# Decode scores: which cached row and which query stand on which partition

## The chip, the cores and the metric

The kernel runs on one core of a Trainium2 chip. The metric is the device time of one execution in microseconds (us); lower is better. A core has five engines that run side by side: TensorE (PE in the profile, its weight loads PEld), VectorE (DVE), ScalarE (ACT), GpSimd (POOL) and SyncE (SP). Each engine takes its instructions in one fixed order, and a waiting instruction holds everything behind it. In this kernel SP issues all data transfers, which 16 DMA engines carry out.

## What is computed

The reference is one inference step of a hybrid layer: a prompt of 1024 rows, and 8 decode requests of 4 new rows each, with 1024 cached key and value rows per request. The part that the change touches is the attention of the new rows to the cache:

```
DILATED_PATTERNS = ((128, 1), (512, 4), (2048, 16))
def _dilated_gather(q, k_all, v_all, window, dil):
    offs = jnp.arange(window // dil + 1) * dil
    idx = (l_ - t_ + jnp.arange(t_))[:, None] - offs[None, :]
    ...
    s = jnp.einsum('bthe,btkhe->bhtk', q, kg) * (HEAD_DIM ** -0.5)
    ...
    o = jnp.einsum('bhtk,btkhe->bthe', p, vg)
def _sample_attention(q, k, v, k_past, v_past):
    ...
    return _combine([_dilated_gather(q, k_all, v_all, w, d) for w, d in DILATED_PATTERNS])
```

Query j (0 to 3) sees keys at distances 0, d, 2d and so on, so with a dilation of 4 or 16 each of the four queries has cached rows of its own: rows j, j+4, j+8, ... among the last 512, and rows j, j+16, ... among the first 512.

## The kernel before

**Stages.** About the first 100 us load and normalise the input. Up to about 320 us the state-space branch runs, with blocks of the input projection between its steps. From 320 to about 540 us come the gated unit of that branch (PE line 748, DVE lines 754 and 755, ACT lines 753, 757 and 759, POOL line 760), the decode scores against the cached keys, and the last three blocks of the input projection (6, 10 and 11; PE line 313, 144 multiplications each; a block's weights come by line 219 and are split by ACT line 141 and DVE line 142). From about 542 us the prompt attention runs, with the decode values and the output projection between its steps, and the rest is the last output projection and the final norm.

**Decode scores.** A loop over the 8 requests (line 818) loads for each request b six tiles of 128 partitions by 512 floats, 256 KB each:

- line 791, tile 0: the last 128 cached key rows. PE transposes it (line 822) and multiplies it with all four queries (lines 828 and 829).
- line 835, `dq`: the four queries of the request, each repeated on 32 partitions.
- line 793, tile 1: the rows of dilation 16, four query classes of 32 rows.
- line 797, tiles 6 to 9: the rows of dilation 4, four query classes of 32 rows in each tile.

Tiles 1 and 6 to 9 go to `dot`: POOL multiplies the tile with `dq` (line 802), and DVE sums each head's 64 products into `scd` (line 803). `query j` has to stand in `dq` on the partitions on which its own rows stand in the tile: before, query j is on partitions 32j to 32j+31.

**Buffers.** The cached tiles share three buffers (`ct`), `dq` has one. So the load of a tile waits until the tile three places ahead of it has been used, and the load of the next request's queries waits until the fifth product of this request is done. All loads, and the stores of other stages, stand in SP's one order.

**What follows.** When all of `scd` is there, PE transposes it (lines 914 and 929), DVE copies it into `sc` in the order query by key (lines 921 and 931), a softmax runs over it (lines 958 to 969), PE turns the weights back (lines 979 and 1008), and the constant `sel3` (line 1543) keeps on each partition only the query that belongs there. The decode values (`values_ops`) load the cached value rows with the same function `cache_tile`: lines 791, 793 and 795.

**What sets the order.** Up to line 866 a scheduler of the framework orders each engine's instructions from estimated durations; from line 868 on a planner (`Plan`) does so with costs and due times written in the code. Waits are fixed when the program is built.

## Time and profile before

| | us |
|---|---|
| median of 3 runs | 816.28 |
| lowest and highest | 814.58, 818.41 |
| the profiled execution's own time | 816.68 |
| its span in the trace | 814.8 |

The profile is of one execution. A row of an engine tells where it was busy and what released it after it had been idle; "DMA ct<-in_cache_k_dram" as a releaser means that the transfer of a cached key tile landed last. In windows, the DMA share is the mean busy share of the 16 DMA engines. The granted clock is TensorE's: 1.00 is 2.4 GHz, 0.50 is 1.2 GHz. Times are counted from the span's start. The chain of waits follows the work that ended last back through what released it; a DMA piece in it lasts from issue to landing.

### The profile page before, as it was taken

Reading aid. Unit: us, or ns where it says so; the run is one execution under the profiler, and the core shown is the slowest. Engines: PE = TensorE matmul, PEld = TensorE weight load, DVE = VectorE, ACT = ScalarE, POOL = GpSimd, SP = SyncE. Lnnn points to the kernel's source line nnn. Section 1 sums busy time; section 2 is a strip of 40 time slices with the busy share of each in tenths; the row PEclk is TensorE's granted clock in tenths of the full one; section 3 lists DMA queues with packets and bytes.
Section 4 is the critical chain, followed back from the end, with each engine's and each line's share of the span. In section 5 each row is a group of like instructions: output and inputs, shape, how many; then the busy total and the mean of one; then the engine's idle time right before and its main releaser. Section 6 shows DMA issues by size and latency. Waiting matters only on the chain.

```text
span 814.8 us, 12780 instructions
## 1 busy us (share of the span) xinstructions
PE 703.5 (86%) x4286; PEld 634.6 (78%) x4286; DVE 561.2 (69%) x1249; ACT 363.3 (45%) x814; POOL 347.0 (43%) x315
## 2 busy tenths in 40 slices
PE   7999989598989999587767668989989999989996
PEld 6999878588978899576767657867757777778896
DVE  5995787879786762444435355649789999996286
ACT  6653244223425244322212222228667787772163
POOL 2506663544654410133433334016567687740022
PEclk9999999798999999796898878989999999999999
DMA  8424142322332444554434354368898788305423
GB/s 282 162 79 139 37 135 85 119 63 67 110 123 93 156 132 147 151 143 160 127 119 142 114 175 139 108 183 243 251 254 247 218 234 242 101 6 181 132 84 130
DMA packets 77362, 118.38 MB, mean 145 GB/s; under 512 B 14544, under 2 KB 42704, under 8 KB 77296
## 3 DMA queue, kind: packets, MB, share of 16 engines
q1 hardware_dynamic: 77296, 117.56, 46.8%
q8 instruction: 34, 0.56, 0.3%
q14 instruction: 32, 0.26, 0.1%
HBM read 85.73 MB, written 30.62 MB: 143 GB/s over the span
## 4 chain that ended last, share of the span: by engine, by line
PE 37%; DMA 28%; DVE 17%; issue 5%; ACT 5%; POOL 4%; SPq 3%; DVEq 0%; POOLq 0%; ACTq 0%
DMA ct<-in_cache_k_dram 13%; PE mm L313 13%; PE mm L293 4%; DMA ct<-in_cache_v_dram 4%; PE ss L293 3%; PE tp L293 3%; PE fo L1418 3%; DMA wst<-in_w_in_dram 3%; PE so L684 2%; POOL dm L802 2%; DVE pm L1269 2%; PE ops L1323 2%; DVE vl L1107 2%; DMA dq<-d_pd 2%; DVE pl L1315 2%
## 5 line engine op out<-in xcount | busy, mean ns | idle before, releaser
L313 PE MATMUL mm<-xT,win 128*128 128x352 f32 x1440 | 262.9, 338 | 23.4 <-DVE eq L380 16.7
L313 PEld LDWEIGHTS mm<-xT,win 128*128 128x128 f32 x1440 | 242.4, 198 | 28.0 <-issue 14.6
L802 POOL TENSOR_TENSOR dm<-ct,dq 128x512 f32<-128x512 f32 x40 | 52.5, 1312 | 124.2 <-DMA ct<-in_cache_k_dram 80.4
L803 DVE TENSOR_REDUCE scd<-dm 128x8 f32<-128x512 f32 x40 | 27.4, 684 | 78.0 <-POOL dm L802 78.0
L748 PE MATMUL ss<-yh,wg 128*128 128x272 f32 (+1 forms) x256 | 56.4, 317 | 19.8 <-DVE z L754 17.1
L1289 POOL TENSOR_SCALAR pm<-pm,rd 128x128 f32<-128x128 f32 (+3 forms) x64 | 52.0, 818 | 39.1 <-DVE rd L1285 27.6
L748 PEld LDWEIGHTS ss<-yh,wg 128*128 128x128 f32 x256 | 46.5, 217 | 22.4 <-DVE z L754 18.7
L142 DVE SCALAR_TENSOR_TENSOR win<-wst,gin,win 128x256 fp32r<-128x256 f32 x96 | 55.2, 617 | 11.0 <-ACT win L141 10.7
L141 ACT ACTIVATE win<-wst,gin 128x256 fp32r<-128x256 f32 x96 | 43.7, 502 | 33.7 <-DMA wst<-in_w_in_dram 29.8
L1281 ACT ACTIVATE pm<-pm,mn 128x128 f32<-128x128 f32 (+3 forms) x64 | 49.2, 770 | 15.3 <-DVE mn L1269 14.9
L1315 DVE TENSOR_TENSOR pl<-tp,ph 128x512 fp32r<-128x512 f32 (+1 forms) x80 | 49.7, 628 | 5.7 <-ACT ph L1312 5.4
L1418 PE MATMUL fo<-wo,gh 128*128 128x512 f32 x192 | 51.1, 408 | 0.0
L293 PE MATMUL mm<-win,xT 128*128 128x256 f32 x384 | 50.4, 286 | 0.1
L1308 PE MATMUL tp<-ident,pm 128*128 128x128 f32 x288 | 47.0, 283 | 1.5 <-DVE mn L1269 1.2
L293 PEld LDWEIGHTS mm<-win,xT 128*128 128x128 f32 x384 | 46.9, 189 | 0.5 <-ACT xT L138 0.4
L1312 ACT ACTIVATE ph<-tp 128x512 fp32r<-128x512 f32 (+1 forms) x80 | 42.9, 543 | 2.7 <-PE tp L1308 1.2
L1269 DVE CUSTOM_DVE_ANT_0 pm<-ss,maskp 128x512 f32<-128x512 f32 (+2 forms) x64 | 36.9, 580 | 9.6 <-DMA qt<-d_q 4.8
L1266 PE MATMUL ss<-ka,qt 128*128 128x512 f32 (+2 forms) x96 | 38.1, 398 | 4.3 <-DMA ka<-d_k 2.4
L1308 PEld LDWEIGHTS tp<-ident,pm 128*128 128x128 f32 x288 | 35.6, 145 | 7.5 <-DVE mn L1269 1.9
L1418 PEld LDWEIGHTS fo<-wo,gh 128*128 128x128 f32 x192 | 35.4, 194 | 6.6
L1103 ACT ACTIVATE vh<-ct 128x512 fp32r<-128x512 f32 x48 | 30.0, 626 | 23.1 <-DMA ct<-in_cache_v_dram 10.9
L379 ACT ACTIVATE eq<-mm 64x352 fp32r<-64x352 f32 (+1 forms) x48 | 21.5, 448 | 41.7 <-DVE eq L380 20.6
(399 smaller groups left out, 1584.7 us busy)
## 6 DMA issues: line engine op xcount, KB each, us to landing
wst<-in_w_in_dram SPq DMA_DIRECT2D x24, 512.0 KB
ct<-in_cache_k_dram SPq DMA_DIRECT2D x48, 256.0 KB
ct<-in_cache_v_dram SPq DMA_DIRECT2D x48, 256.0 KB
xt<-in_x_prompt_dram SPq DMA_DIRECT2D x8, 512.0 KB
wst<-in_w_out_dram SPq DMA_DIRECT2D x8, 512.0 KB
xres<-in_x_prompt_dram SPq DMA_DIRECT2D x8, 512.0 KB
qt<-d_q SPq DMA_DIRECT2D x16, 256.0 KB
qw<-d_q SPq DMA_DIRECT2D x32, 128.0 KB
```

The lines of the kernel that those rows point to most:

```text
L141: S.activation(hi, src, AF.Copy, scale=scale)
L142: V.scalar_tensor_tensor(lo, src, scale, f(hi), op0=OP.mult, op1=OP.subtract)
L293: T.matmul(out, lhs(a, kt), w(b, kt)[:, c0:c0 + cn], start=(n == 0), stop=(n == 3 * ktn - 1))
L313: T.matmul(p, w(b, kt)[:, c * 128:c * 128 + 128], x(a, kt), start=(n == 0), stop=(n == 23))
L748: T.matmul(p, wg[:, b, kt, c:c + 128], yT[a][:, kt, :, :w], start=(i == 0), stop=(i == 11))
L802: GP.tensor_tensor(out=m, in0=kt, in1=qt, op=OP.mult)
L1269: V.tensor_tensor_reduce(out=x.pm[:, 512 * c:512 * c + w], in0=x.p[c][:, :w], in1=maskp[:, (7 - i) * 128 + 512 * c:(7 - i) * 128 + 512 * c ...
L1281: S.activation(x.pm[:, :n], x.pm[:, :n], AF.Exp, scale=-1.0, bias=x.mn[:, nch - 1:nch], accum_out=x.dn)
L1289: a = op(PO, 0.02 + n * 0.0012, lambda: GP.tensor_scalar(x.pm[:, :n], x.pm[:, :n], x.rd, 1.0, op0=OP.mult, op1=OP.mult), pr, [a], give=["rd"])
L1308: T.transpose(x.p[:, n * 128:n * 128 + 128], o.rows[2 * m + u].pm[:, j * 128:j * 128 + 128], ident)
L1315: V.tensor_tensor(out=x.l[:, :w], in0=x.p[:, :w], in1=f(x.h[:, :w]), op=OP.subtract)
L1418: T.matmul(o.f[hf], o.g[u][:, i, k], wo[0][:, j, 2 * u + k, hf * 512:hf * 512 + 512], start=(u + k + n == 0), stop=(u + k + n == 4))
```

## The change

The partitions are renumbered: query j now stands on partitions 4m+j instead of 32j+m. With that,

- line 797 loads the 128 consecutive cached rows of a tile (rows 512+128i to 639+128i for tile 6+i) one after the other, where it loaded the same 128 rows as four classes of 32, each row four rows after the one before it;
- line 793 loads the same 128 rows as before, with the 32 groups m outermost and the class j inside, for the keys and for the values;
- line 835 loads the queries as 32 repeats of the group of four, where it loaded four groups of 32 repeats;
- the copies out of the transposes (lines 920, 928 to 931) and one copy ahead of line 1008 (line 1012) step through their input or output with a stride of four elements, and `sel3` follows.

Number and size of the transfers, the shapes of all instructions on the engines, and the arithmetic are as before. Since the scheduler orders the stage from estimated durations, instructions of the stage stand in another order; outside 320 to 540 us the order on each engine is the same.

```diff
         elif t == 1:
-            SY.dma_start(c, src[b, 0:512, :].rearrange("(m r) c -> r m c", r=16)[0:DS])
+            SY.dma_start(c, src[b, 0:512, :].rearrange("(m r) c -> m r c", r=16)[:, 0:DS])
...
         else:
-            SY.dma_start(c, src[b, 512:1024, :].rearrange("(m r j) c -> m j r c", r=32, j=DS)[t - 6])
+            SY.dma_start(c, src[b, 128 * t - 256:128 * t - 128, :])
...
-        SY.dma_start(qt, d_pd[:, b, 1024:1536].unsqueeze(1).to_broadcast([DS, 32, 512]))
+        SY.dma_start(qt, d_pd[:, b, 1024:1536].unsqueeze(0).to_broadcast([32, DS, 512]))
...
-                out, p = out.rearrange("q j (m r) -> q m j r", r=32), (lambda: o.p.rearrange("q m (j r) -> q m j r", r=32))
+                out, p = out.rearrange("q j (m r) -> q m j r", r=32), (lambda: o.p.rearrange("q m (r j) -> q m j r", j=DS))
...
-            o.p = fo_ps([64, 4, 32])
-            T.transpose(o.p.rearrange("p j m -> p (j m)"), scd[:, 8].rearrange("p b h -> p (b h)"), ident)
+            o.p = fo_ps([64, 32, 4])
+            T.transpose(o.p.rearrange("p m j -> p (m j)"), scd[:, 8].rearrange("p b h -> p (b h)"), ident)
...
-        step(VE, 0.2, lambda: V.tensor_scalar(sc[:, :, 256:288], o.p, 0.125, 0.0, op0=OP.mult, op1=OP.add), give=["fo"])
+        step(VE, 0.2, lambda: V.tensor_scalar(sc[:, :, 256:288], o.p.rearrange("p m j -> p j m"), 0.125, 0.0, op0=OP.mult, op1=OP.add), give=["fo"])
...
-            V.tensor_copy(o.s3.rearrange("p (j m) -> p j m", j=4), sc[:, :, 256:288])
+            V.tensor_copy(o.s3.rearrange("p (m j) -> p j m", j=4), sc[:, :, 256:288])
...
-    sel3 = (np.arange(128)[:, None] // 32 == np.arange(4)[None, :]).astype(np.float32)
+    sel3 = (np.arange(128)[:, None] % 4 == np.arange(4)[None, :]).astype(np.float32)
```

**SP, the loads of the third request.** `ct` are the cached tiles, `dq` the queries, `gt` a gate tile of the gated unit (line 740), `d_k<-eq` a store of block 6. Before:

```order
L793 DMA ct_4541<-in_cache_k_dram 128x1x512
L381 DMA d_k_84<-eq_4871 128x320
L835 DMA dq_4539<-d_pd_91 128x1x512
L797 DMA ct_4546<-in_cache_k_dram 128x1x512
L381 DMA d_k_84<-eq_4900 128x352
L740 DMA gt_4087<-d_gs_88 128x2x128
L381 DMA d_k_84<-eq_4904 128x352
L797 DMA ct_4551<-in_cache_k_dram 128x1x512
L797 DMA ct_4556<-in_cache_k_dram 128x1x512
L740 DMA gt_4120<-d_gs_88 128x2x128
L797 DMA ct_4561<-in_cache_k_dram 128x1x512
L791 DMA ct_4566<-in_cache_k_dram 128x512
```

After:

```order
L793 DMA ct_4541<-in_cache_k_dram 128x1x512
L740 DMA gt_4087<-d_gs_88 128x2x128
L835 DMA dq_4539<-d_pd_91 128x1x512
L797 DMA ct_4546<-in_cache_k_dram 128x512
L381 DMA d_k_84<-eq_4900 128x352
L381 DMA d_k_84<-eq_4904 128x352
L740 DMA gt_4120<-d_gs_88 128x2x128
L797 DMA ct_4551<-in_cache_k_dram 128x512
L797 DMA ct_4556<-in_cache_k_dram 128x512
L740 DMA gt_4154<-d_gs_88 128x2x128
L797 DMA ct_4561<-in_cache_k_dram 128x512
L791 DMA ct_4566<-in_cache_k_dram 128x512
```

The gate tiles stand one place earlier against the cached tiles, and the cached tiles of line 797 have the plain form of line 791's.

**PE, the transposes of the last request's tile 0** (`ct_4762`), between the multiplications of block 10 (`mm`). Before:

```order
L313 MATMUL mm_5122<-xT0_97,win_5088 128x352 x2
L313 MATMUL mm_5122<-xT1_98,win_5088 128x352
L822 MATMUL tp_4764<-ident_73,ct_4762 128x128 x4
L763 MATMUL so_3782<-ones_69,acc_4230 128x1 x2
L313 MATMUL mm_5151<-xT0_97,win_5067 128x352 x2
```

After:

```order
L313 MATMUL mm_5210<-xT1_98,win_5076 128x352
L313 MATMUL mm_5210<-xT0_97,win_5079 128x352
L822 MATMUL tp_4764<-ident_73,ct_4762 128x128 x4
L313 MATMUL mm_5210<-xT0_97,win_5079 128x352
L313 MATMUL mm_5210<-xT1_98,win_5079 128x352
```

They moved behind 61 further multiplications of line 313 (1261 of the program's 1440 stand ahead of them, where 1200 did).

**PE, the last transposes of the scores** (lines 914 and 929), before (`mm_5239` is the last sixth of block 10, `mm_5412` and `mm_5442` the first two of block 11):

```order
L313 MATMUL mm_5239<-xT0_97,win_5088 128x352 x2
L313 MATMUL mm_5239<-xT1_98,win_5088 128x352
L914 MATMUL ss_5322<-ident_73,scd_3749 64x128 x2
L929 MATMUL ss_5328<-ident_73,scd_3749 64x128
L313 MATMUL mm_5412<-xT0_97,win_5387 128x352 x2
```

After:

```order
L313 MATMUL mm_5442<-xT0_97,win_5396 128x352
L914 MATMUL ss_5322<-ident_73,scd_3749 64x128
L313 MATMUL mm_5442<-xT0_97,win_5396 128x352
L313 MATMUL mm_5442<-xT1_98,win_5396 128x352
L313 MATMUL mm_5442<-xT0_97,win_5399 128x352
L929 MATMUL ss_5328<-ident_73,scd_3749 64x128
```

Line 929 moved from 1296 to 1333 multiplications of line 313 ahead of it, and the turn of the weights behind the softmax (line 979) from 1392 to 1416, so that 83 multiplications lie between the two where 96 did.

## Rows read from the trace of the kernel before

**Rows 1.** The page's chain of waits: share of the span, by engine, by line

```profile
PE 37%; DMA 28%; DVE 17%; issue 5%; ACT 5%; POOL 4%; SPq 3%; DVEq 0%; POOLq 0%; ACTq 0%
DMA ct<-in_cache_k_dram 13%; PE mm L313 13%; PE mm L293 4%; DMA ct<-in_cache_v_dram 4%; PE ss L293 3%; PE tp L293 3%; PE fo L1418 3%; DMA wst<-in_w_in_dram 3%; PE so L684 2%; POOL dm L802 2%; DVE pm L1269 2%; PE ops L1323 2%; DVE vl L1107 2%; DMA dq<-d_pd 2%; DVE pl L1315 2%
```

**Rows 2.** Windows: length; PE, PEld, DVE, ACT, POOL busy; clock, DMA share, GB/s

```profile
560.00:740.00 180.00, 166.49 (x982) 133.76 (x981) 160.03 (x399) 132.02 (x284) 117.00 (x105) 0.98 0.69 196
220.00:300.00 80.00, 74.02 (x504) 68.82 (x503) 60.08 (x106) 34.48 (x81) 31.06 (x27) 1.00 0.39 125
100.00:300.00 200.00, 176.24 (x1150) 164.49 (x1150) 158.40 (x250) 77.40 (x183) 96.02 (x79) 0.95 0.34 108
320.00:510.00 190.00, 137.83 (x852) 130.97 (x851) 86.93 (x180) 49.95 (x115) 62.92 (x53) 0.84 0.48 147
```

**Rows 3.** Groups of instructions, 326 to 505 us: busy, mean ns, idle before, releasers

```profile
L802 POOL TENSOR_TENSOR dm<-ct,dq 128x512 f32<-128x512 f32 x40 | 52.5, 1312 | 124.2 <-DMA ct<-in_cache_k_dram 80.4 <-DMA dq<-d_pd 32.7 <-DVE dm L139 6.7
L803 DVE TENSOR_REDUCE scd<-dm 128x8 f32<-128x512 f32 x39 | 26.7, 684 | 74.1 <-POOL dm L802 74.1
```

**Rows 4.** Waits of PE, 326 to 505 us: total, times, longest

```profile
PE tp L822 <- DMA ct<-in_cache_k_dram: 24.9, 6, 7.9
PE ss L748 <- DVE z L754: 17.1, 7, 5.8
```

**Rows 5.** Pieces of the chain of waits: start, us, what

```profile
329.92 12.83 DMA ct<-in_cache_k_dram
...
398.57 6.36 DMA dq<-d_pd
...
430.13 7.72 DMA ct<-in_cache_k_dram
```

**Rows 6.** Short windows, columns as in rows 2

```profile
431.00:433.00 2.00, 2.00 (x12) 2.00 (x11) 0.74 (x3) 1.35 (x4) 0.70 (x1) 0.50 0.26 102
...
472.00:474.00 2.00, 0.00 (x0) 0.00 (x0) 2.00 (x3) 0.43 (x1) 0.94 (x1) 1.00 0.26 102
...
563.00:566.00 3.00, 3.00 (x19) 2.27 (x18) 1.87 (x8) 2.68 (x8) 3.00 (x5) 1.00 1.05 336
```

**Rows 7.** SP's timeline: the query loads of the first and the last request

```profile
326.54 0.58 SPq L835 DMA_DIRECT2D dq<-d_pd  x1
...
480.64 0.54 SPq L835 DMA_DIRECT2D dq<-d_pd  x1
```

**Rows 8.** SP's issues by line: ns min/median/max, first and last start

```profile
L797 SPq DMA_DIRECT2D ct<-in_cache_k_dram x32: 536/554/666, 329.3 to 492.5; - x32
L791 SPq DMA_DIRECT2D ct<-in_cache_k_dram x8: 328/338/468, 326.0 to 474.4; - x8
```

**Rows 9.** Pieces of the chain of waits, loads of other forms

```profile
506.09 2.02 DMA nk<-d_pd
...
547.91 4.47 DMA ct<-in_cache_v_dram
```

**Rows 10.** PE's timeline: start, us, line, tile, count [idle before, releaser]

```profile
507.16 0.30 PE L929 MATMUL ss<-ident,scd 128*64 128x128 f32 x1 [0.28 <-DVE sc L921]
...
521.50 4.14 PE L313 MATMUL mm<-xT,win 128*128 128x352 f32 x24 [0.19 <-DVE ge L372]
525.57 0.70 PE L979 MATMUL ss<-ident,sc 64*128 64x64 f32 x8
...
542.54 0.45 PE L1266 MATMUL ss<-ka,qt 128*128 128x128 f32 x1 [2.39 <-DMA ka<-d_k]
```

**Rows 11.** The copies of the transposed scores: ns min/median/max, first and last start

```profile
L921 DVE TENSOR_SCALAR sc<-ss x2: 673/674/675, 506.4 to 511.7; 64x512 f32<-64x512 f32 x2
```

**Rows 12.** Waits for cached value tiles, 545 to 740 us: total, times, longest

```profile
ACT vh L1103 <- DMA ct<-in_cache_v_dram: 10.9, 10, 2.4
PE fo L1113 <- DVE vl L1107: 4.1, 7, 1.1
```

**Rows 13.** Window in which line 1480 repeats one row on 128 partitions

```profile
747.70:749.00 1.30, 1.30 (x12) 1.24 (x11) 0.75 (x1) 1.15 (x1) 0.00 (x0) 1.00 0.55 224
```

## The prediction

> **What bounds the kernel now.** The profiled execution took 816.7 us, 1.9 of them outside the span of 814.8; the median of the three runs is 816.28, so a sum made against the profiled execution stands 0.4 above the median. I read the chain of waits first. Beside PE's own work its largest entry is one transfer, the cached key tiles, 13% of the span (106 us), with 2% for the queries [rows 1]. Next comes the stretch in which these loads run. In the windows PE is busy for 137.8 of the 190 us from 320 to 510, at a mean clock of 0.84; from 560 to 740 it is busy for 166 of 180 at 0.98 [rows 2]. So the slack is in the stretch with the decode scores: 52 us of idle PE, and a clock that falls with it.
>
> Who waits there for whom? POOL stood idle for 124 us ahead of its 40 products, 80.4 of them for key tiles and 32.7 for queries; DVE then stood for 74.1 us at the sums behind the products [rows 3]. DVE's queue is in order, so the gated unit's DVE steps are held too, and PE waits 17.1 us for them; 24.9 us more PE waits for tile 0 itself [rows 4]. These are 42 of the 52 us. Eleven pieces of the chain are key tiles, from 12.83 us to 7.72 us, and a query load is 6.36 [rows 5]. That is long for 256 KB, and the reason is in the short windows: with nothing but such loads in flight, the DMA share is 0.26 and the rate 102 GB/s, at two places; later, with other loads, it is 1.05 and 336 GB/s [rows 6]. A share of 0.26 is four of the sixteen engines. The loads whose outermost dimension is the four query classes (lines 793, 797 and 835) are carried by four engines only. At 102 GB/s one takes 2.57 us of them, and a request has six: 15.4 us. The query loads of the first and the last request are 154.1 us apart, 22.0 us for each of seven steps [rows 7]. So those four engines are taken for 70% of the time by these loads alone, and every other load, tile 0 and weights too, has a part on them and queues behind.
>
> **The change part by part.**
>
> *The transfers.* Line 797 gets exactly the form of line 791, 128 rows in one dimension; lines 793 and 835 get an outermost dimension of 32. If all 16 engines carry them, a load's 2.57 us become 0.64, and 15.4 us per request become 3.9. The stretch's mean share of 0.48 over 190 us is 91 us of work for all engines [rows 2], 68% of 135 us (the stretch's length below), so the DMA engines no longer bound it. How long will such a load take from issue to landing? No row has it alone. From below: 2.02 us for a small load with nothing else in flight; from above: 4.47 us for 256 KB of value rows in line 791's form, in a crowded moment [rows 9]. I take the middle, 3.3, since the stretch will be busy but not full.
>
> The Trainium skill, page "DMA: Bandwidth & Descriptors", section "Why a DMA increments its semaphore by 16 and not by 1", says that a transfer runs on the largest number of engines up to 16 that divides the slowest dimension of both sides. The share of 0.26 agrees for the four classes; for the new query load, a repeat of 32, no run here shows it yet. The same page's section "Anatomy of one DMA" gives 2.0 us and bytes over 436 GB/s for transfers that GpSimd issues, 2.6 us here as an estimate; with that the loop below would be 13.1 us and the sum 760.
>
> *The loop of one request.* After the last product of a request the queries can be loaded; then two products run (1.31 us each [rows 3]), the second one's buffer takes the last tile, it lands, its product runs, and the next queries are loaded: 2.62 + 0.1 + landing + 1.31 + 0.1 + landing. With today's 7.72 and 6.36 this is 18.2 us; the trace has 22.0, so 3.8 us are lost beside it (POOL's other sums, SP's queue). With 3.3 twice it is 10.7, with the same loss 14.5; with 4.47 it is 16.9, with 2.02 it is 12.0. The stretch has 190 - 8 x 22.0 = 14 us besides. So the loop would let it last 14 + 8 x 14.5 = 130 us (110 to 149).
>
> *PE's own work.* 137.8 us at a mean clock of 0.84 is 115.8 us at full clock, an estimate from the window. PE does not reach that. From 100 to 300, with the same multiplications between DVE and POOL steps, it was busy for 88% at 0.95, together 0.84; from 220 to 300 for 92.5% at 1.00 [rows 2]. There DVE is busy for 79% and 75%; here it would be 87 of 135 us, 64%. I take 0.88: 115.8 / 0.88 = 131.6 us (125 to 139).
>
> So two limits come to nearly the same, 130 and 131.6. Two pipelines of one pace, tied by in-order queues, cost each other something: I add 3 us (0 to 17, the upper end being the loop's 149). **The stretch: 135 us instead of 190, minus 55.**
>
> *The tail.* From line 929 to line 979 the trace has 18.4 us (507.16 to 525.57), the softmax, with PE's multiplications beside it. In the new order 83 of them lie between, at 4.14 us for 24, so 14.3 us [rows 10]. PE may wait for the difference, 4.1 us; since DVE has less other work there I take 2 (0 to 4.1). The prompt attention starts at 542.54 [rows 10] behind it, and shifts as a whole.
>
> *What costs nothing.* The copies out of the transposes step by four elements: two of 0.67 us [rows 11], one of them with the stride, and two others a quarter as large. If a stride doubled them it would be about 1 us on the softmax's path; no row shows a stride's price, a gain has no reason; 0 (0 to 1). The new queue place on SP: the issue of line 797 took 554 ns where the plain form takes 338 [rows 8], 32 times, 6.9 us less of SP; SP waits for buffers most of the time, so 0 (a gain of 0 to 6.9). The gate tiles move ahead of the cached tiles by one place, a load that only DVE's gated unit uses; 0. The eight value loads of line 793: the attention's waits for value tiles are 10.9 us on ACT, and 4.1 us on PE behind them [rows 12]; PE is 92% busy there, so 0 (a gain of 0 to 4.1).
>
> **Sum:** 816.7 - 55 + 2 = 763.7, against the median 763.3; I say 764, with 750 to 774 as the forecast's own range.
>
> **The rivals.**
>
> *The loop still ends last.* All loads now use all engines, so a K tile meets weights and gate tiles on each of them, and lands in 4.47 us or later, as the value tile did [rows 9]. The loop is then 16.9 us, the stretch 149: 816.7 - 41 + 2 = 778; at a landing of 6 us the loop is 19.9 and the stretch 173, 802. For it: SP's one queue and three buffers remain. Against it: the share falls to 68%.
>
> *PE becomes dense.* With the stalls gone the clock stays at its upper level, 2.4 GHz, and the stretch nears 115.8 to 123 us: 744 to 752. For it: from 220 to 300 the clock is 1.00 and PE at 92.5% [rows 2]. Against it: that is the best that an interleaved stretch here reaches, and it would be 125 us.
>
> *The loads are not spread*, because lines 793 and 835 keep a destination of the old shape, or the repeat counts otherwise. Line 797's new form is line 791's and excludes it for four of the six; if the queries stay at 6.36 the loop is 17.6 us, 779, inside the first rival. That nothing at all changes, 816, I hold for hardly possible.
>
> *Slower: the queries read one place at once.* In the new order all 16 engines start on the same four rows of 2 KB, where each of four had one row. If these reads go one after another, 128 x 0.08 us (2 KB at a quarter of 102 GB/s) is 10.2 us and a landing of about 12.3: the loop is 2.62 + 0.1 + 3.3 + 1.31 + 0.1 + 12.3 + 3.8 = 23.5 us, 1.5 more than now for each of eight requests, 12 us: 829. It decides from a landing of 10.8 us on. Against it: line 1480 repeats one row on 128 partitions in one transfer, and the window in which it runs has 224 GB/s [rows 13], far from one engine's 25.
>
> **How the numbers follow.** Forecast 0.58; the loop ends last 0.21; PE dense 0.14; not spread at all 0.03; slower by the queries 0.04, half of it milder and below today's time. A range of 740 to 788 takes in the forecast, most of the dense case and the loop up to a landing of about 5 us, some 0.86. What this kernel's measurement can tell from no change is about 0.5%, 4 us. Faster by more: 0.58 + 0.21 + 0.14 + 0.02 = 0.95; within it 0.03; slower 0.02.
>
> **What would show it.** In the new profile the short windows should not show 0.26 with 102 GB/s any more; the query loads should be 14 to 17 us apart; POOL's wait for tiles and queries should fall from 113 us to about 40; DVE's wait at line 803 from 74 to below 25; PE's wait at line 822 to almost nothing; PE should be busy for over 85% of the stretch with a clock above 0.93; the first score multiplication of the prompt (line 1266) should come at about 490 instead of 542.5, and what follows should last as before, 272 us. Steps of the query loads near 17 to 20 us with PE idle mean the first rival; query landings over 10 us the last one; an attention that gets longer when it starts earlier would be a cost that I have not counted.

## The result, and the profile after

The changed kernel takes 748.66 us (median of 4 runs, 746.96 to 753.76) against 817.35 for the kernel before in the same series: a ratio of 0.917, 95% interval 0.912 to 0.923. The profiled execution took 747.05 us with a span of 745.3, which is 69.6 less than before. The forecast was 764, with 750 to 774 as its own range; the time lies just below that, among the 744 to 752 of the rival "PE becomes dense", and in the range of 740 to 788. Medians here and below are of all runs of a kernel, while ratios leave out single slow runs (one each of eight_engines, old_order_all_16 and, at 2079 us, before_more_buffers).

The page's chain of waits after, by engine and by line:

```profile
PE 54%; DVE 17%; DMA 14%; issue 5%; ACT 4%; POOL 3%; SPq 2%; DVEq 0%; POOLq 0%; ACTq 0%
PE mm L313 19%; PE mm L293 5%; PE fo L1418 4%; PE tp L293 3%; PE ss L293 3%; DMA ct<-in_cache_v_dram 3%; PE ops L1323 3%; PE ss L748 3%; PE so L684 3%; DMA ct<-in_cache_k_dram 2%; DVE vl L1107 2%; DMA wst<-in_w_in_dram 2%; DMA u<-d_u 2%; PE
```

The cached key tiles fell from 13% of the span to 2%, and the queries no longer show; PE's share rose from 37% to 54% [rows 1]. The stretch from 320 us to the first score multiplication of the prompt (line 1266), first before, then after; in windows the columns are length, PE, PEld, DVE, ACT and POOL busy, clock, DMA share, GB/s:

```profile
320.00:542.50 222.50, 166.51 (x1014) 156.54 (x1012) 105.43 (x221) 57.02 (x133) 62.92 (x53) 0.86 0.46 143
```

```profile
320.00:479.10 159.10, 147.04 (x1014) 140.50 (x1013) 113.91 (x221) 57.51 (x133) 67.16 (x53) 0.99 0.65 200
```

Both windows hold 1014 matmuls of PE. PE's idle time fell from 56.0 to 12.1 us, and its busy time from 166.5 to 147.0, because the granted clock rose from 0.86 to 0.99 (1.00 is 2.4 GHz). So 43.9 us of the 63.4 are waits that went, and 19.5 are the same work at the higher clock.

That the loads went from four engines to 16 can be read from the page's number of packets, before and after:

```profile
DMA packets 77362, 118.38 MB, mean 145 GB/s; under 512 B 14544, under 2 KB 42704, under 8 KB 77296
```

```profile
DMA packets 78034, 118.38 MB, mean 159 GB/s; under 512 B 15216, under 2 KB 43376, under 8 KB 77968
```

The bytes are the same; 672 packets under 512 B came in, 12 for each of the 56 loads whose form changed (six key or query loads and one value load for each of eight requests). Twelve is 16 - 4, and eight_engines has 14768, which is 4 more per load, 8 - 4: one small packet for each engine that carries a part. The other runs fit to the packet: tiles_on_16 has 14928 (32 loads changed), tiles_on_4 14832 (24), queries_on_4 and values_on_4 15120 (48).

The groups of the products after (busy, mean ns, idle before, releasers), and PE's waits for tile 0:

```profile
L802 POOL TENSOR_TENSOR dm<-ct,dq 128x512 f32<-128x512 f32 x40 | 54.8, 1381 | 55.3 <-DMA ct<-in_cache_k_dram 22.6 <-DMA dq<-d_pd 14.8 <-DVE zd L771 6.9
L803 DVE TENSOR_REDUCE scd<-dm 128x8 f32<-128x512 f32 x40 | 27.1, 680 | 19.3 <-POOL dm L802 19.2
```

```profile
PE tp L822 <- DMA ct<-in_cache_k_dram: 0.4, 1, 0.4
```

POOL waits 37.4 us for tiles and queries (17.4 of them once, ahead of the first product, as 22.4 were before) where it waited 113.1, DVE 19.2 where it waited 74.1 [rows 3], and PE's 24.9 us at line 822 [rows 4] are 0.4. SP's timeline with the query loads of the first and the last request, and two short windows with many loads in flight:

```profile
325.77 0.61 SPq L835 DMA_DIRECT2D dq<-d_pd  x1
...
434.88 0.52 SPq L835 DMA_DIRECT2D dq<-d_pd  x1
```

```profile
360.00:362.00 2.00, 2.00 (x15) 2.00 (x14) 1.09 (x2) 0.95 (x2) 0.61 (x2) 1.00 0.93 309
412.00:414.00 2.00, 2.00 (x19) 2.00 (x18) 1.11 (x2) 0.00 (x0) 1.90 (x3) 1.00 1.01 377
```

One request takes (434.88 - 325.77) / 7 = 15.6 us where it took 22.0 [rows 7]. The pieces of the chain of waits that are cached key tiles or queries (start, us from issue to landing, what) are four, none above 5.69 us, where one was 12.83 [rows 5]:

```profile
326.63 5.69 DMA ct<-in_cache_k_dram
333.87 5.52 DMA ct<-in_cache_k_dram
379.50 4.80 DMA ct<-in_cache_k_dram
390.76 4.80 DMA dq<-d_pd
```

PE's timeline between the scores and the prompt attention (start, us, line, tile, count, idle before and its releaser), to be read against [rows 10]:

```profile
452.13 0.27 PE L929 MATMUL ss<-ident,scd 128*64 128x128 f32 x1
...
455.06 11.87 PE L313 MATMUL mm<-xT,win 128*128 128x352 f32 x72 [0.78 <-DVE ge L372]
...
466.97 0.70 PE L979 MATMUL ss<-ident,sc 64*128 64x64 f32 x8
...
479.12 0.30 PE L1266 MATMUL ss<-ka,qt 128*128 128x128 f32 x1 [1.51 <-DMA ka<-d_k]
```

The copies of the scores, two of them now with a strided output or input, take what they took [rows 11]:

```profile
L921 DVE TENSOR_SCALAR sc<-ss 64x512 f32<-64x512 f32 x2 | 1.3, 672 | 0.0
L931 DVE TENSOR_SCALAR sc<-ss 64x128 f32<-64x128 f32 x1 | 0.3, 273 | 0.0
```

### The profile page after: what moved, and what is told of

Same layout as the page of the kernel before. It is cut to its first block, busy times and chain, and to the rows that moved or that the text cites. A ratio compares the mean times of both kernels' runs of the same rounds, so it can differ in the third digit from the quotient of the medians.

```text
span 745.3 us, 12787 instructions
## 1 busy us (share of the span) xinstructions
PE 683.2 (92%) x4286; PEld 622.2 (83%) x4286; DVE 568.7 (76%) x1249; ACT 364.2 (49%) x814; POOL 352.4 (47%) x315
## 4 chain that ended last, share of the span: by engine, by line
PE 54%; DVE 17%; DMA 14%; issue 5%; ACT 4%; POOL 3%; SPq 2%; DVEq 0%; POOLq 0%; ACTq 0%
PE mm L313 19%; PE mm L293 5%; PE fo L1418 4%; PE tp L293 3%; PE ss L293 3%; DMA ct<-in_cache_v_dram 3%; PE ops L1323 3%; PE ss L748 3%; PE so L684 3%; DMA ct<-in_cache_k_dram 2%; DVE vl L1107 2%; DMA wst<-in_w_in_dram 2%; DMA u<-d_u 2%; PE ss L1266 2%; DVE pm L1269 2%
## 5 line engine op out<-in xcount | busy, mean ns | idle before, releaser
L313 PE MATMUL mm<-xT,win 128*128 128x352 f32 x1440 | 255.0, 332 | 22.0 <-DVE eq L380 14.9
L313 PEld LDWEIGHTS mm<-xT,win 128*128 128x128 f32 x1440 | 236.7, 193 | 25.7 <-issue 15.4
L802 POOL TENSOR_TENSOR dm<-ct,dq 128x512 f32<-128x512 f32 x40 | 54.8, 1381 | 55.3 <-DMA ct<-in_cache_k_dram 22.6
L142 DVE SCALAR_TENSOR_TENSOR win<-wst,gin,win 128x256 fp32r<-128x256 f32 x96 | 58.9, 654 | 6.8 <-ACT win L141 6.4
L748 PE MATMUL ss<-yh,wg 128*128 128x272 f32 (+1 forms) x256 | 50.3, 293 | 2.0 <-DVE wg L139 0.7
L141 ACT ACTIVATE win<-wst,gin 128x256 fp32r<-128x256 f32 x96 | 43.3, 501 | 14.1 <-DMA wst<-in_w_in_dram 12.1
L748 PEld LDWEIGHTS ss<-yh,wg 128*128 128x128 f32 x256 | 40.8, 192 | 3.1 <-DVE z L754 1.2
L803 DVE TENSOR_REDUCE scd<-dm 128x8 f32<-128x512 f32 x40 | 27.1, 680 | 19.3 <-POOL dm L802 19.2
L1266 PE MATMUL ss<-ka,qt 128*128 128x512 f32 (+2 forms) x96 | 37.2, 389 | 3.8 <-DMA qt<-d_q 2.0
L748 PE MATMUL ss<-yl,wg 128*128 128x272 f32 (+1 forms) x128 | 36.9, 290 | 1.6 <-DVE yl L139 1.6
```

What stands on the lines that cost most here:

```text
L142: V.scalar_tensor_tensor(lo, src, scale, f(hi), op0=OP.mult, op1=OP.subtract)
L313: T.matmul(p, w(b, kt)[:, c * 128:c * 128 + 128], x(a, kt), start=(n == 0), stop=(n == 23))
L748: T.matmul(p, wg[:, b, kt, c:c + 128], yT[a][:, kt, :, :w], start=(i == 0), stop=(i == 11))
L802: GP.tensor_tensor(out=m, in0=kt, in1=qt, op=OP.mult)
L1266: T.matmul(x.p[c][:, :w], q[:, i % 4 * 128:i % 4 * 128 + 128], o.ka[:, 512 * c:512 * c + w], start=(m == 0), stop=(m == 1))
```

## The experiments

The theory to be tested: a load whose outermost dimension is 4 is carried by four of the 16 engines, these four set the pace of the stretch before, and 16 engines per load are the whole gain. Its rivals: the order that the scheduler makes for the new form; rows that follow each other in memory; one of the three lines alone; or latency, which more buffers would hide as well. The table has all runs. "Four-engine time" counts the time for which the six loads of a request in question take the four engines that carried them before: 2.57 us for each on four engines, 1.28 on eight, 0.64 on 16. Ratios are to the kernel before in the same series, whose medians were 817.35, 813.88, 816.37 and 818.67. The profiled executions give the step of the query loads, the start of line 1266, and the time from there to the end.

| kernel | four-engine time, us | step, us | L1266 at | from there | median, us | ratio to before [95%] |
|---|---|---|---|---|---|---|
| before | 15.4 | 22.0 | 542.5 | 272.3 | 817.35 | 1 |
| before_more_buffers | 15.4 | (two buffers) | 541.0 | 270.6 | 814.86 | 0.996 [0.992, 1.000] |
| tiles_on_4 | 11.6 | 19.4 | 519.2 | 264.7 | 785.68 | 0.966 [0.962, 0.969] |
| old_order_16 (the same loads) | 11.6 | 19.5 | 522.4 | 264.4 | 786.87 | 0.966 [0.962, 0.970] |
| tiles_on_16 | 7.7 | 18.6 | 501.8 | 272.7 | 776.08 | 0.953 [0.948, 0.957] |
| eight_engines | 7.7 | 16.5 | 495.2 | 265.7 | 763.66 | 0.935 [0.930, 0.941] |
| queries_on_4 | 5.8 | 16.8 | 489.7 | 263.5 | 756.22 | 0.926 [0.919, 0.934] |
| values_on_4 | 3.9 | 15.6 | 479.2 | 272.3 | 757.23 | 0.926 [0.923, 0.929] |
| the changed kernel | 3.9 | 15.6 | 479.1 | 266.2 | 748.66 | 0.917 [0.912, 0.923] |
| after_again (the same) | 3.9 | 16.0 | 485.9 | 264.7 | 750.12 | 0.917 [0.914, 0.920] |
| old_order_all_16 | 3.9 | 14.4 | 479.7 | 266.9 | 748.52 | 0.915 [0.912, 0.918] |
| strided_16 | 3.9 | 15.7 | 476.6 | 264.0 | 743.14 | 0.912 [0.908, 0.916] |
| after_two_queries | 3.9 | (two buffers) | 473.6 | 266.2 | 741.15 | 0.906 [0.901, 0.911] |
| after_more_buffers | 3.9 | (two buffers) | 473.2 | 264.7 | 740.94 | 0.905 [0.901, 0.910] |

**One part undone, one part alone.** In tiles_on_4 line 797 has its form of before, the rest is new:

```diff
-            SY.dma_start(c, src[b, 128 * t - 256:128 * t - 128, :])
+            SY.dma_start(c, src[b, 512:1024, :].rearrange("(m r j) c -> m j r c", r=32, j=DS)[t - 6])
```

> The changed kernel with line 797 in its form of before (outermost dimension 4), lines 793 and 835 new; order as before. Rows of tiles 6 to 9 then stand on partitions 32j+m while the queries stand on 4m+j, so their scores are of wrong pairs. Theory 'engines': four of six loads stay on four engines: 4 x 2.57 + 2 x 0.64 = 11.6 of 15.4 us, loop 15.6 + 6.4 x (11.6 - 3.9) / (15.4 - 3.9) = 19.9 us, 817 - 8 x 2.1 = 800; the value loads of line 793 on 16 engines may give another 0 to 6 us in the attention, so 790 to 806. Rival 'the tiles alone count': 810 to 817. Rival 'the queries alone count' (the one-buffer link of the loop): 750 to 770.

Measured 785.68, 4 us under the expected range: the step came nearly as computed (19.4 for 19.9), the value loads seem to have given the upper end of what was allowed for them, and the kernel before was at 813.88 in this series, not at 817. A short window of it with three four-engine loads and one gate tile in flight still has the share of [rows 6]:

```profile
380.00:382.00 2.00, 2.00 (x17) 2.00 (x16) 0.62 (x2) 0.49 (x2) 0.59 (x1) 1.00 0.26 100
```

The next run was meant to have all loads on 16 engines in the old order. Its dimensions were written with the class j outermost all the same, so line 797 loads exactly what it loads in tiles_on_4; the expectation below describes another kernel, and the run only repeats the one above (786.87 for 785.68). The question was taken up again in old_order_all_16.

```diff
-            SY.dma_start(c, src[b, 128 * t - 256:128 * t - 128, :])
+            SY.dma_start(c, src[b, 128 * t - 256:128 * t - 128, :].rearrange("(m j) c -> j m c", j=4))
```

> The changed kernel, with the 128 consecutive rows of line 797 described as 32 groups of 4 rows, so that the dimensions stay apart as in the kernel before. The order on every engine is then that of the kernel before (apart from the seven strided copies), while all cached and query loads have an outermost dimension of 32. Theory 'engines': the gain comes from 16 engines in place of 4 for each of these loads and the new order has no part in it: 745 to 755 us, no stretch at 0.26 and 102 GB/s, query loads 15 to 16.5 us apart. Rival 'order': the new order, which the scheduler chose for the plain form, brings most of the gain: 790 to 816, query loads over 19 us apart. Rival 'issue': SP's shorter issue of the plain form (327 for 554 ns, 32 times, 7.3 us in all) shows in the time: 752 to 757.

In tiles_on_16 the kernel before gets line 797's new form alone:

```diff
-            SY.dma_start(c, src[b, 512:1024, :].rearrange("(m r j) c -> m j r c", r=32, j=DS)[t - 6])
+            SY.dma_start(c, src[b, 128 * t - 256:128 * t - 128, :])
```

> The kernel before with line 797 alone changed to 128 consecutive rows; lines 793 (keys and values) and 835 stay on an outermost dimension of 4; the order is that of the changed kernel. Scores of tiles 6 to 9 are of wrong pairs. Theory 'engines': 4 x 0.64 + 2 x 2.57 = 7.7 us of the four engines per request, loop 15.6 + 6.4 x (7.7 - 3.9) / (15.4 - 3.9) = 17.7 us, 750 + 8 x 2.1 = 767, and without whatever the value loads on 16 engines give in the attention 767 to 773; in all 755 to 785. Rival 'the tiles alone count' or 'order': 745 to 754. Rival 'the queries alone count': 795 to 817.

Measured 776.08, inside the range of "engines" and over 20 us from "the tiles alone count". Its order is the changed kernel's, so the order alone brings at most this run's gain. The two parts add up within the noise: 813.88 - 776.08 = 37.8 us for the tiles of line 797, 813.88 - 785.68 = 28.2 us for lines 793 and 835, together 66.0, and all parts gave 816.37 - 750.12 = 66.3 in another series. The step is 18.6 and not 17.7, most likely because the loads left on four engines include the one that stands in the link of the one query buffer: the chain of waits of tiles_on_16 is full of it, and POOL waits for it (total, times, longest):

```profile
366.56 7.51 DMA dq<-d_pd
383.85 7.60 DMA dq<-d_pd
399.98 8.23 DMA dq<-d_pd
```

```profile
POOL dm L802 <- DMA dq<-d_pd: 50.2, 7, 9.9
```

**The dose.** In eight_engines each of the three lines has an outermost dimension of 8:

```diff
-            SY.dma_start(c, src[b, 0:512, :].rearrange("(m r) c -> m r c", r=16)[:, 0:DS])
+            SY.dma_start(c, src[b, 0:512, :].rearrange("(m r) c -> r m c", r=32)[0:8])
...
-            SY.dma_start(c, src[b, 128 * t - 256:128 * t - 128, :])
+            SY.dma_start(c, src[b, 512:1024, :].rearrange("(m r j) c -> m j r c", r=16, j=8)[t - 6])
...
-        SY.dma_start(qt, d_pd[:, b, 1024:1536].unsqueeze(0).to_broadcast([32, DS, 512]))
+        SY.dma_start(qt, d_pd[0, :, 1024:1536].unsqueeze(1).to_broadcast([8, 16, 512]))
```

> Lines 793, 797 and 835 with an outermost dimension of 8 (8 groups of 16 rows; for the queries the eight requests' rows of query 0, each 16 times), order as in the kernel before. Rows and queries then stand on other partitions than the copies and sel3 take them from, so scores are of wrong pairs; sizes and work are the same. Theory 'engines': eight engines carry each load, 1.28 us of them for 256 KB; alone in flight they show a DMA share near 0.5 and 200 GB/s. The loop of a request, 22.0 us at 2.57 us a load and 15.6 at 0.64, should be in proportion: 15.6 + 6.4 x (1.28 - 0.64) / (2.57 - 0.64) = 17.7 us, and with 8 of them the time 750 + 8 x 2.1 = 767; 752 to 785, the lower end if PE's own work ends last before the loop does. Rival 'consecutive rows' (the rows of a group lie 8 rows apart here): as slow as before, 805 to 817.

Measured 763.66, between four and 16 engines, near the 767 of the proportion; the step is 16.5 where 17.7 was computed. A short window while such loads are in flight (with two stores and a gate tile):

```profile
400.00:402.00 2.00, 2.00 (x18) 2.00 (x18) 0.00 (x0) 0.00 (x0) 0.99 (x1) 1.00 0.52 184
```

A share of 0.26 with 100 GB/s on four, 0.52 with 184 on eight, 0.93 to 1.01 with 309 to 377 with loads on all 16: with the counts of packets above, the outermost dimension sets how many engines carry a load. This is the rule that the Trainium skill states on its page "DMA: Bandwidth & Descriptors", section "Why a DMA increments its semaphore by 16 and not by 1": the largest number up to 16 that divides the outermost dimension of both sides. The sizes tried here, 4, 8 and 32 or 128, agree with it.

**The order, and rows that follow each other.** In old_order_all_16 line 797 has 32 classes of 4 rows, which keeps three dimensions and with them the old order; in strided_16 it loads rows four apart in one dimension, with the changed kernel's order to the letter.

```diff
-            SY.dma_start(c, src[b, 128 * t - 256:128 * t - 128, :])
+            SY.dma_start(c, src[b, 512:1024, :].rearrange("(m r j) c -> m j r c", r=4, j=32)[t - 6])
```

> The changed kernel with line 797 loading the same 128 rows of a tile as 32 classes of 4 rows (32 rows apart), so three dimensions stay apart and the scheduler makes the order of the kernel before, while all loads have an outermost dimension of 32. Rows of tiles 6 to 9 stand on other partitions, so their scores are of wrong pairs. Theory 'engines': 16 engines carry every load, the loop is as in the changed kernel: query loads 15 to 16.5 us apart, 746 to 757 us. Rival 'order': the old order holds the stretch back whatever the transfers, and eight engines in this order are already at its floor: 760 us or more, query loads 16.5 us apart or more. Rival 'issue': SP's longer issue of a form with three dimensions (554 for 327 ns, 32 times) shows in full: 7 us above the changed kernel.

```diff
-            SY.dma_start(c, src[b, 128 * t - 256:128 * t - 128, :])
+            SY.dma_start(c, src[b, 506 + t:1024:4, :])
```

> The changed kernel with line 797 loading 128 rows that lie four apart (every fourth row of the last 512, in the form of line 795), all in one dimension; the order on every engine is exactly that of the changed kernel. Each tile then holds rows of one class on all partitions, so its scores are of wrong pairs. Theory 'engines': the distance between rows of 2 KB has no price: within 4 us of the changed kernel on the same chip. Rival 'consecutive rows': part of the gain is due to rows that follow each other in memory: slower than the changed kernel by 8 us or more, and key tiles land later than there.

> The changed kernel, unaltered, as the reference for the three other runs on the same chip: 744 to 754 us, first score multiplication of the prompt (line 1266) near 479, and 264 to 267 us from there to the end.

On this chip the changed kernel has 750.12, old_order_all_16 748.52 and strided_16 743.14. So the order has no measurable part in the gain, and rows of 2 KB that lie four or 32 rows apart show no cost against consecutive ones; strided_16 is if anything faster, but the intervals overlap. Nor does SP's longer issue of the form with three dimensions matter, 547 ns at the median in old_order_all_16 against 364 (lines by SP, in ns min/median/max, first and last start):

```profile
L797 SPq DMA_DIRECT2D ct<-in_cache_k_dram x32: 535/547/609, 328.0 to 434.7; - x32
```

```profile
L797 SPq DMA_DIRECT2D ct<-in_cache_k_dram x32: 327/364/1397, 328.5 to 443.6; - x32
```

**The value tiles.** The part behind line 1266 had become 6.1 us shorter, which the prediction had put at 0. In values_on_4 the value tiles of line 793 alone go back to four engines, in the changed kernel's order:

```diff
-            SY.dma_start(c, src[b, 0:512, :].rearrange("(m r) c -> m r c", r=16)[:, 0:DS])
+            SY.dma_start(c, src[b, 0:512, :].rearrange("(m r) c -> m r c", r=16)[:, 0:DS] if src is ck else src[b, 0:512, :].rearrange("(m r) c -> r m c", r=16)[0:DS])
```

> The changed kernel with the value tiles of line 793 alone in their form of before (outermost dimension 4); the order on every engine is exactly that of the changed kernel. The value rows then stand on 32j+m while the weights stand on 4m+j, so the values of this pattern are weighted wrongly. Theory 'value tiles': the 6 us by which the part from line 1266 to the end became shorter (272.3 to 266.2) come from these eight loads: that part is 270 to 274 us again, ACT again waits some 8 to 11 us for value tiles, and the time is 4 to 9 us above the changed kernel on the same chip; the stretch ahead of it is unchanged. Rival 'chance or clock': the part differs by less than 2 us from the changed kernel's.

Measured 757.23, 7.1 above the changed kernel; the stretch ahead is unchanged (line 1266 at 479.2) and the part behind it is 272.3 us again. In the table all kernels with these loads on four engines have 270.6 to 272.7 there, all others 263.5 to 266.9. ACT's waits for the value tiles are back (total, times, longest), 7.4 us where the kernel before has 10.9 [rows 12] and the changed kernel none:

```profile
ACT vh L1103 <- DMA ct<-in_cache_v_dram: 7.4, 7, 2.5
```

But it is not in PE's waits that the time shows. From line 1266 to the end, with 1332 matmuls in both, values_on_4 first, then the changed kernel on the same chip (after_again):

```profile
479.20:751.50 272.30, 250.06 (x1332) 208.92 (x1332) 215.25 (x544) 171.82 (x374) 140.01 (x124) 0.95 0.60 182
```

```profile
485.90:750.60 264.70, 242.69 (x1332) 204.03 (x1332) 216.02 (x544) 171.78 (x374) 140.70 (x124) 0.97 0.59 186
```

Of the 7.6 us, 7.4 are longer busy time of PE and 0.2 longer idle time; the medians of the two kernels differ by 7.1. Most of the 7.4 goes with the clock: at full clock the two would be 250.06 x 0.95 = 238 and 242.69 x 0.97 = 235 us. Why the clock is lower when these tiles come late is open.

**What sets the stretch now?** If PE does, a slower loop costs little and a freer loop gains little. In queries_on_4 the query load alone goes back to four engines; after_two_queries has a second query buffer, after_more_buffers also a fourth tile buffer; each of the last two gets an order of its own.

```diff
-        SY.dma_start(qt, d_pd[:, b, 1024:1536].unsqueeze(0).to_broadcast([32, DS, 512]))
+        SY.dma_start(qt, d_pd[:, b, 1024:1536].unsqueeze(1).to_broadcast([DS, 32, 512]))
```

> The changed kernel with the query load of line 835 alone in its form of before (outermost dimension 4); the order on every engine is exactly that of the changed kernel. The queries then stand on 32j+m, the rows on 4m+j, so these scores are of wrong pairs. The query load sits in the one-buffer link of the loop, and 2.57 us of four engines replace 0.64. Theory 'PE sets the stretch and the loop has slack': the loop's 15.6 us become up to 17.5, of which PE's stretch takes little: query loads 15.6 to 16.5 us apart, 748 to 756 us. Rival 'the loop still ends last': each of eight requests pays 1.1 us (in proportion to the transfers of a request, 6.4 x 1.9 / 11.5) to 1.9 us: 758 to 766. Rival 'the queries alone were the cost': 775 or more.

```diff
-        return dk([128, 512], "dq", bufs=1)
+        return dk([128, 512], "dq", bufs=2)
```

> The changed kernel with two query buffers for one, tile buffers as they are, in an order of its own. POOL waits 14.8 us for queries in the stretch. Theory 'PE sets the stretch': 742 to 752, POOL's waits for queries below 5 us without effect on the time. Rival 'the one query buffer holds the loop': 8 us or more faster, below 742.

```diff
-        c = dk([128, 512], "ct", bufs=3) if fin[0] else gk([128, 512], "ct", bufs=CT)
+        c = dk([128, 512], "ct", bufs=4) if fin[0] else gk([128, 512], "ct", bufs=CT)
...
-        return dk([128, 512], "dq", bufs=1)
+        return dk([128, 512], "dq", bufs=2)
```

> The changed kernel with two query buffers for one and four tile buffers for three, in an order of its own. Theory 'PE sets the stretch': PE is busy 147.0 of the 159.1 us from 320 to 479 at 0.99, and only waits of the loop within the other 12 us can go: 742 to 752. Rival 'the loop still ends last': the product loop speeds up and the stretch with it, by 8 us or more: below 742, with PE over 95% busy in it.

Queries_on_4 took 756.22 with a step of 16.8, between the two theories: the loop has little slack. POOL's waits for queries are 35.9 us for 14.8:

```profile
POOL dm L802 <- DMA dq<-d_pd: 35.9, 7, 7.9
```

With a second query buffer these waits are gone, and the time is 741.15; with a fourth tile buffer too it is 740.94. Both lie just on the rival's side of 742, and against after_again's 0.914 to 0.920 the interval of after_more_buffers, 0.901 to 0.910, stands apart; the interval of strided_16, which has one query buffer, overlaps it at 0.908 to 0.916. So the one query buffer most likely still held PE; what part the new orders have in it is not shown. The stretch of after_more_buffers:

```profile
320.00:473.20 153.20, 146.28 (x1026) 141.97 (x1024) 114.07 (x222) 58.91 (x137) 66.96 (x53) 0.99 0.66 208
```

PE is busy for 95.5% of it at 0.99, where the changed kernel had 92.4%; 6.9 us of idle time are left there. This version, the change and a second query buffer, beats both kernels by some 1% and 9%; the fourth tile buffer adds nothing that these runs can tell.

**Would buffers have done without the change?** The same edit of two lines as in after_more_buffers, in the kernel before:

```diff
-        c = dk([128, 512], "ct", bufs=3) if fin[0] else gk([128, 512], "ct", bufs=CT)
+        c = dk([128, 512], "ct", bufs=4) if fin[0] else gk([128, 512], "ct", bufs=CT)
...
-        return dk([128, 512], "dq", bufs=1)
+        return dk([128, 512], "dq", bufs=2)
```

> The kernel before, loads unchanged on four engines, with two query buffers for one and four tile buffers for three; the scheduler makes an order of its own for it. Theory 'the four engines are full': from 320 to 510 all 16 engines together were busy 0.48 of 190 us, 1459 us; the loads in question are 8 x 15.4 us on each of four engines, 493 us; the rest, 966 us over 16 engines, is 60 us on each, so each of the four is taken for 123 + 60 = 183 of 190 us, and more loads in flight cannot help: 805 to 822. Rival 'latency': the waits come from loads issued too late (one query buffer, three tile buffers), and 16 engines only shorten that latency: with the buffers the loop falls towards 15.4 to 18 us and the time to 770 to 790.

Measured 814.86, a gain of 0.4%. The chain of waits shows what became of loads that could now start earlier, and the window runs from the first to the last load of line 797:

```profile
354.61 10.89 DMA dq<-d_pd
367.65 8.75 DMA ct<-in_cache_k_dram
383.77 11.68 DMA ct<-in_cache_k_dram
398.97 12.05 DMA ct<-in_cache_k_dram
```

```profile
328.00:475.00 147.00, 99.34 (x627) 97.59 (x628) 63.09 (x119) 35.81 (x82) 55.50 (x48) 0.81 0.44 143
```

Loads stay longer in flight. By the semaphore records of the trace, which show when each part of a load had landed, the eight query loads landed 7.15 to 13.31 us after their issue (median 12.03), where they took 6.36 to 7.98 before (6.65); the tiles of line 797 have a median of 10.19 for 9.20. Part of the wait for a buffer has become time in flight. By the expectation's arithmetic, 0.44 of 147 us for 16 engines is 1035 us; less the 493 of the loads in question, 34 us are left for each engine, and with 123 the four have 157 us of work in 147: an estimate that is higher than can be, but puts them near full.

The loop did gain something: the last load of line 797 came 20 us earlier than before (472.5 for 492.5). That did not reach the time: in the order made for these buffers 192 multiplications of line 313 stand behind line 929 where 144 did, and PE's waits for tile 0 grew from 24.9 us [rows 4] to 34.0. So the run shows that buffers alone, in the order that comes with them, bring next to nothing; what they would bring in the old order is not shown.

```profile
PE tp L822 <- DMA ct<-in_cache_k_dram: 34.0, 6, 8.0
```

## Why the prediction was right, and where it was off

**What bound the kernel: right.** Six loads of a request on four of 16 engines: the counts of packets show the four, and the dose shows that the number of engines sets the time. Neither the order, nor consecutive rows, nor one line alone carries the gain, and more buffers did not bring it; how full the four engines were is an estimate. One reading was loose: at 431 us a gate tile is in flight beside the four-engine loads [rows 6], at 472 us nothing else is.

**The loop: 14.5 us forecast, 15.6 measured**, inside 12.0 to 16.9, but partly by luck, because the formula's path was no longer the loop's. It pays two landings of 3.3 us for each request, the queries' and the last tile's. The query loads landed 3.78 to 5.24 us after their issue (median 4.50, by the semaphore records), near the upper bound of 4.47; the stretch's DMA share had risen from 0.46 to 0.65. The last tile landed after 2.54 to 4.39 us, and in seven of eight requests half a microsecond or more before POOL came to it. Before the change each of the 32 products with tiles of line 797 started 0.13 to 0.16 us after its tile had landed. POOL's timeline for one request of the changed kernel, whose queries were issued at 376.95 and the next at 390.76, has a wait for the queries and none for a tile:

```profile
382.31 1.27 POOL L802 TENSOR_TENSOR dm<-ct,dq 128x512 f32<-128x512 f32 x1 [5.20 <-DMA dq<-d_pd]
384.38 3.98 POOL L802 TENSOR_TENSOR dm<-ct,dq 128x512 f32<-128x512 f32 x3 [0.80 <-DVE scd L803]
...
389.02 1.29 POOL L802 TENSOR_TENSOR dm<-ct,dq 128x512 f32<-128x512 f32 x1
```

On the mean of the seven steps, 5.0 us pass from the issue of the queries to the first product, 9.9 over the five products (6.9 of them busy, at 1.38 each), and 0.7 until the next issue: 15.6. The estimate that the prediction drew from the Trainium skill, page "DMA: Bandwidth & Descriptors", section "Anatomy of one DMA", 2.6 us for such a load, is what the quickest tiles took (2.54) and far from the queries' 4.50; its sum, 760, lay nearer to the result for other reasons.

**The stretch and the tail: -53 forecast, -63.4 measured**, at line 1266. This is the step that was mis-sized. Up to line 929 the forecast was -55, and the traces have 507.16 and 452.13, which is 55.0 less; but that agreement is partly luck, since the new order has put 37 further multiplications ahead of line 929 (6.4 us at 24 in 4.14). The prediction counted them where the tail becomes shorter than the softmax, and neither in the stretch nor as work that leaves the tail. Over both together, PE's work before is 166.51 x 0.86 = 143.2 us at full clock. At the 0.88 taken it would last 162.7 us, and with 3 for the coupling and 2 for the tail 167.7, so line 1266 at 488. It lasted 159.1, of which PE's work at full clock is 147.04 x 0.99 = 145.6, a density of 0.915. Three terms, then:

- *0.88 was too low.* Without the query buffer's waits PE reaches 146.28 x 0.99 / 153.2 = 0.945 (after_more_buffers). The denser of the two reference windows, 0.925 from 220 to 300 [rows 2], was the better guide, although DVE is as busy here as there (113.91 of 159.1 us, 72%, where the prediction had 64%).
- *The coupling of 3 us was probably too small.* With a second query buffer line 1266 starts at 473.2 and 473.6; the five profiles with all key and query loads on 16 engines and one query buffer have 476.6 to 485.9, which is 3 to 13 us later, an estimate from single executions in different orders.
- *The tail's 2 us didn't come.* From line 929 to line 979 it is 14.8 us, the multiplications' own time; PE waited 0.78 us there, for DVE's line 372 and not for the softmax.

**The value loads: 0 (a gain of 0 to 4.1) forecast, -6.1 measured**, 7.1 in values_on_4. The bound failed because it was taken from PE's waits behind the value tiles; nearly all of the price stands in PE's busy time, most of it with a lower clock, where no wait names it. Without it the time would have been about 755.

**What costs nothing: right.** The strided copies out of the transposes (672 for 674 ns, 273 for 270; the one copy of line 1012 took 266 for 209), the gate tiles' place, and SP's shorter issue, which old_order_all_16 does without and loses nothing.

**The rivals.** "The loop still ends last" was wrong as a forecast of 778, but its mechanism is there in small: queries_on_4 and after_two_queries lie 6 us above and 9 us below after_again, which ran on another chip. "PE becomes dense" came nearest, but its time is partly luck: its stretch of 115.8 to 123 us would have put line 1266 earlier by 65 to 72 us, where 63.4 were measured; the total reaches 744 to 752 only by the 6.1 us of the value loads, which that rival did not have. "Not spread" is excluded by the counts of packets. Its price for queries left on four engines should have been 783 by its own loop of 17.6 us (14 + 8 x 17.6 is 155), not 779, and queries_on_4, which is that kernel, took 756.22: its step is 16.8, but line 1266 came 53 us earlier than before, where 33 follow from that sum, and the value loads gave the rest. "Slower by the queries" is excluded: a query load of 32 repeats landed in at most 5.24 us here and 6.13 in after_again, far from 10.8.

**The list of signs** held in all but three points: the start of line 1266 (479 for 490) and the part behind it (266 for 272), the two misses above, and the window with a share of 0.26. The changed kernel has such a window too, with all its loads on 16 engines:

```profile
401.00:403.00 2.00, 2.00 (x16) 2.00 (x16) 1.94 (x5) 1.44 (x5) 2.00 (x3) 1.00 0.26 99
```

Cut finer it looks different. Here are two half microseconds of it, and two of the window at 472 us of the kernel before:

```profile
401.00:401.50 0.50, 0.50 (x6) 0.50 (x6) 0.50 (x2) 0.00 (x0) 0.50 (x2) 1.00 0.86 332
402.00:402.50 0.50, 0.50 (x5) 0.50 (x4) 0.47 (x2) 0.50 (x3) 0.50 (x1) 1.00 0.00 0
```

```profile
472.00:472.50 0.50, 0.00 (x0) 0.00 (x0) 0.50 (x2) 0.43 (x1) 0.00 (x0) 1.00 0.26 102
473.00:473.50 0.50, 0.00 (x0) 0.00 (x0) 0.50 (x2) 0.00 (x0) 0.44 (x1) 1.00 0.25 98
```

In the changed kernel a nearly full moment is followed by an idle one; before, the share stays at 0.25 to 0.29. Only a share that stays tells of four engines.

## What to carry to other kernels

Where the profile's chain is full of one load's landings, look for a short window with only such loads in flight: a share that sticks at a fraction of the 16 engines through windows of half a microsecond, like 0.26, says that the form of the load and not its size is the price. The page's count of small packets confirms it. Here renumbering the partitions so that the outermost dimension became 32 or 128 cost nothing that could be measured, with a stride in later copies. More buffers brought next to nothing ahead of the change; after it a second buffer for the queries is worth some 1%. And when an order changes, count the work on both sides of a landmark before crediting time to it.

## What was not expected of the hardware

- 128 rows of 2 KB that lie four or 32 rows apart loaded as well as consecutive ones: 743.14 and 748.52 against 750.12 us for the whole kernel.
- Eight loads of 256 KB on four engines among loads on all 16 cost 7.1 us in a stretch in which PE is over 91% busy, almost none of it as a wait of PE: 7.4 us longer busy time in the profiles, with a clock of 0.95 for 0.97.
- With more loads in flight on the four engines each landed later: the query loads had a median of 12.03 us in before_more_buffers, where it was 6.65 before.
- Two profiled executions of the changed kernel, of two series, differ by 5.3 us (745.3 and 750.6), all of it ahead of line 1266 (479.1 and 485.9), with 0.99 and 0.96 as the clock in that stretch.
